# Two transformer blocks with experts on one core: conditioning on VectorE, joined biases, gate in the rows, and a changed start and end of the second experts

## The chip, the cores and the metric

The kernel runs on one core of one Trainium2 chip. The metric is the time of one execution on the device, in microseconds (us). PE is the matrix engine, PEld its weight load, DVE the vector engine, ACT the scalar engine, POOL the general engine, and SP the engine that here only issues transfers.

## What is computed

`reference` runs `first_block` and then `second_block` on 256 tokens of width 1024 (the first block also on 256 context tokens). Cut to what the change touches:

```python
def first_block(x, c, ctx, c_ctx, ...):
    mod_lat = split(silu(c) @ w_mod + b_mod, 6)          # 1024 x 6144
    mod_ctx = split(silu(c_ctx) @ w_mod + b_mod, 6)
    h = rmsnorm(x) * (1 + mod_lat[1]) + mod_lat[0]
    x = x + mod_lat[2] * token_mixer(h, ...)              # attention + gated recurrence
    h = rmsnorm(x) * (1 + mod_lat[4]) + mod_lat[3]
    x = x + mod_lat[5] * moe_ffn(h, ...)                  # 32 experts, top 4 of 32
    return rmsnorm(x, final_norm_g)

def expert(xb, e):                                        # inside moe_ffn
    gu = xb @ w_gate_up[e] + b_gate_up[e]                 # 1024 x 2048
    act = swiglu(gu)
    return act @ w_down[e] + b_down[e]                    # 1024 x 1024

def second_block(x, c, ...):
    mod = silu(c) @ w_ada + b_ada                         # 1024 x 6144
    x = x + gt1 * mixer2(modulate(rmsnorm(x), sh1, sc1))
    x = x + gt2 * hier_moe(modulate(rmsnorm(x), sh2, sc2))  # 32 experts of 256, top 2
    shf, scf = split(silu(c) @ w_ada_f + b_ada_f, 2)      # 1024 x 2048
    return modulate(rmsnorm(x), shf, scf)
```

The last block's context rows are not needed, so the first experts work on the 256 tokens alone.

## The kernel before

All weights are read once from device memory, in tiles of 128 x 2048 fp32 (1 MB) that `wload` (L311) issues from SP into a ring of slots; a tile can be issued when the last reader of its slot is done. Outside the expert stages the ring has five slots. Five stages follow one another.

**Block 1** runs the projections of the token mixer, four pairs of recurrence heads, and attention. `tproj` takes one weight tile: ACT casts it to a high part (`wsh`, L495), DVE takes the rest (`wsl`, L496), and PE multiplies three times (L508 to L510). Work items stand in a queue, `self.q`; `step` runs the first and issues the loads of the first two. Conditioning rows are items of the same queue: `mod` loads two tiles and `modrow` multiplies the condition vector with them on PE (16 matmuls into `modps`, L367), and DVE adds the result to `rowall` (L369). Twenty such rows are listed in `MODS1` and mixed between the projections: twelve go with the head pairs, eight with the last group of gate projections, `g8s`. Four more, for the final norm (`wadaf`), are made at the start of block 2. `mod_cols` turns rows into columns at the end of block 1. `bcast_rows` (L425) copies a row to all partitions by one fp32 matmul.

**The first experts**, `moe1`, go through 32 experts with up to 64 tokens each. An expert takes eight tiles of `wgu` and four of `wdn`. `expert1a` multiplies the gathered tokens (`gu`, L1327), adds the bias by four fp32 matmuls of 32 rows (L1402) and makes the activation; `expert1b` multiplies with `wdn` (`y`, L1358) and adds its bias by two more. `combine` weighs y (`yhi` on ACT, L1236, `ylo` on DVE, L1237), puts the rows back to tokens on PE (`co`, L1248), multiplies by the gate on DVE (L1253) and adds to x (L1254). The next expert's `gu` matmuls are interleaved with the last steps of the present one. The ring has 14 slots here: five of the main ring, one and eight of two other pools. After expert 11 `overflow` asks whether any expert has more tokens than its places; nine tiles of the next expert are issued ahead of this check. The branch isn't taken with this data.

**Block 2** is the second mixer. **The second experts**, `moe2`, run 32 small experts (three 1 MB tiles each: `w1e`, `w3e`, `w2e`), eight with fixed places first, then in an order by their counts: `sorted_places` computes that order as `inv`, and SP reads it into registers (`TENSOR_LOAD`, L1461) before it can issue the loads of a sorted expert. An overflow check lies behind the eight fixed experts. The sums over experts stay in four banks of PSUM (`sum`, L1562).

**The end** (L1607 to L1616) multiplies the sums by the gate, adds x, takes the mean of squares (ACT, L1609), the inverse root through a logarithm and an exponential (L431, L432), scales, adds the shift and writes out.

```python
        for k in range(8):                        # cut: one gu chain of expert1a, then its biases
            nc.tensor.matmul(gu[j][64 * s:64 * s + 64, :], g[:, k, c0:c0 + 64],
                             w[:, ...], start=(k == 0), stop=False)
        for j in range(2):
            for s in range(2):
                bias(gu[j][64 * s:64 * s + 64, :], 0, 1024 * s + 512 * j)
```

Of the kernel before, what the change touches and what calls it, by code (L numbers as in the profile page):

```python
# [23 lines left out]
MODS1 = [(1, j) for j in range(4, 12)] + [(2, j) for j in range(12)]  # L24
NWS, NU, NV = 8, 32, 20
NWR = 5
# [5 lines left out]
def _cols(a):  # L32
# [8 lines left out]
VOFF = {}  # L41
# [14 lines left out]
def _khalf(w):  # L56

    t = w.shape[1] // 512
    return np.ascontiguousarray(w.reshape(2, 4, 128, t, 512).transpose(3, 0, 2, 1, 4)).reshape(2 * t, 128, 2048)
# [62 lines left out]
def layout(i):  # L122
# [117 lines left out]
class Ker:  # L240
    def __init__(self, tc, d, out, dbg=None, stop=None, start=1):
        self.tc, self.nc, self.d, self.out = tc, tc.nc, d, out
        self.dbg = dbg or {}
        self.stop, self.start = stop, start
# [5 lines left out]
    def run(self):  # L250
        with ExitStack() as es:
            tc = self.tc
            self.cp = es.enter_context(tc.tile_pool(name="const", bufs=1))
            self.wp = es.enter_context(tc.tile_pool(name="wts", bufs=NWR))
# [3 lines left out]
            own = self.own = [(self.wp, "w")]  # L258
# [3 lines left out]
            if self.start <= 1:  # L262
                with tc.tile_pool(name="t1late", bufs=1, side="right") as pl, tc.tile_pool(name="t1", bufs=1) as p:
                    self.early = lambda n: p.tile([128, 512], F32, name=n, tag="u", bufs=NU)
                    self.consts()
                    route = self.block1(p, pl, xtile)
            else:
                self.early = lambda n: self.cp.tile([128, 512], F32, name=n)
                self.consts()
                self.x1 = xtile("x").rearrange("p a (b n) -> p (a b n)", b=1).rearrange("p (b n) -> p b n", b=2)  # L270
                self.nc.sync.dma_start(self.x1, self.d['xin'])
                self.add(*(self.mod(2, j) for j in range(12)))
                self.drain()
                self.mod_cols((12, 10, self.mcol2[:, 0:40]))
# [1956 lines left out]
```

## Time and profile before

| | us |
|---|---|
| median of 3 runs | 2112.69 (2109.07 to 2114.51) |
| profiled execution | 2111.07 |
| its span | 2109.3 |
| PE busy in the span | 1945.5 (92%) |
| DVE busy | 896.0 (42%) |
| ACT busy | 511.6 (24%) |

The mean granted clock of PE is 0.963. The span is the time from the first to the last instruction that the profiler recorded. Busy shares are means over stages that have different limits, so the stages have to be read apart. Matmuls are pipelined: a row that says 600 ns for one does not mean that PE issued the next one 600 ns later; where rows stand back to back, the distance of their starts is the price.

### The profile page before, as it was taken

How to read it: one execution, taken by the hardware profiler on the slowest of the kernel's cores; microseconds unless marked ns; L12 is line 12 of the kernel's file. 1: busy time of each engine (PE TensorE's matmuls, PEld its weight loads, DVE VectorE, ACT ScalarE, POOL GpSimd, SP SyncE). 2: the span in 40 equal slices, each digit the busy share in tenths (PEclk: the TensorE clock that was granted, in tenths of full speed). 3: DMA queues.
4: the chain of work that ended last, by engine and by line, in shares of the span. 5: the costliest groups of instructions: out<-in, count | busy, mean ns of one | idle time of the engine just before them, and what ended most of it. 6: DMA issues, size and time to landing. Idle time of an engine off the chain costs nothing. (4 is left out here: it accounts for less than half of the span.)

```text
span 2109.3 us, 30791 instructions
## 1 busy us (share of the span) xinstructions
PE 1945.5 (92%) x12860; PEld 1114.6 (53%) x12861; DVE 896.0 (42%) x1727; ACT 511.6 (24%) x893; POOL 63.3 (3%) x66
## 2 busy tenths in 40 slices
PE   5999999999899999989999999999969998899785
PEld 3888788877733333333333333333338997764331
DVE  5666754445423233332323333242378574421112
ACT  3433454344300001000000100000035543311011
POOL 0000000000000000000000000000032201000000
PEclk9999999999999999989999999999989999989897
DMA  9255636732699999979999999999873133289895
GB/s 362 81 219 201 227 126 258 278 111 80 262 415 427 411 427 416 427 295 407 426 427 427 426 427 427 426 427 427 365 292 124 62 121 103 114 370 420 360 425 226
DMA packets 95272, 646.11 MB, mean 306 GB/s; under 512 B 11668, under 2 KB 12692, under 8 KB 19220
## 3 DMA queue, kind: packets, MB, share of 16 engines
q1 hardware_dynamic: 93296, 642.79, 74.9%
q8 instruction: 104, 1.70, 0.3%
q10 hardware_dynamic: 1828, 1.26, 0.2%
q14 instruction: 44, 0.36, 0.0%
HBM read 642.96 MB, written 1.05 MB: 305 GB/s over the span
## 5 line engine op out<-in xcount | busy, mean ns | idle before, releaser
L1327 PE MATMUL gu<-w,gT 128*64 128x512 f32 x2048 | 481.2, 597 | 0.0
L1327 PEld LDWEIGHTS gu<-w,gT 128*64 128x64 f32 x2048 | 148.1, 137 | 278.1 <-issue 263.1
L1358 PE MATMUL y<-w,aT 128*64 128x512 f32 x1024 | 229.4, 601 | 0.4
L496 DVE TENSOR_TENSOR wsl<-w,wsh 128x1024 fp32r<-128x1024 f32 (+1 forms) x141 | 168.6, 1205 | 97.6 <-ACT wsh L495 97.3
L495 ACT CAST wsh<-w 128x1024 fp32r<-128x1024 f32 (+1 forms) x141 | 143.4, 1030 | 169.0 <-PE tp L509 97.4
L1337 DVE TENSOR_SCALAR act<-gu 128x256 f32<-128x256 f32 x64 | 27.2, 425 | 307.5 <-PE gu L1402 304.2
L1237 DVE SCALAR_TENSOR_TENSOR ylo<-y,sw,yhi 128x512 fp32r<-128x512 f32 x52 | 39.0, 751 | 264.5 <-ACT yhi L1236 264.0
L1358 PEld LDWEIGHTS y<-w,aT 128*64 128x64 f32 x1024 | 71.9, 139 | 148.6 <-issue 143.7
L508 PE MATMUL tp<-hs,wsh 128*128 128x256 f32 (+1 forms) x424 | 139.7, 329 | 0.0
L510 PE MATMUL tp<-hs,wsl 128*128 128x256 f32 (+1 forms) x424 | 134.3, 317 | 4.1 <-DVE wsl L496 4.1
L509 PE MATMUL tp<-hs,wsh 128*128 128x256 f32 (+1 forms) x424 | 133.6, 315 | 0.0
L1529 PE MATMUL ab<-w,gT 128*32 128x256 f32 (+1 forms) x1024 | 99.8, 415 | 17.4 <-DMA w<-in_w1e_dram 10.8
L1236 ACT ACTIVATE yhi<-y,sw 128x512 fp32r<-128x512 f32 x52 | 35.8, 688 | 300.9 <-PE y L1402 239.9
L1253 DVE TENSOR_TENSOR gated<-co,gtb 128x512 f32<-128x512 f32 x128 | 88.3, 690 | 34.6 <-PE co L1248 27.5
L1339 ACT ACTIVATE sge<-act 128x512 f32<-128x512 f32 x32 | 20.1, 630 | 331.3 <-DVE act L1337 331.3
L508 PEld LDWEIGHTS tp<-hs,wsh 128*128 128x128 f32 x424 | 81.7, 193 | 16.3 <-issue 4.9
L1254 DVE TENSOR_TENSOR x<-x,gated 128x512 f32<-128x512 f32 x128 | 88.3, 690 | 3.3
L510 PEld LDWEIGHTS tp<-hs,wsl 128*128 128x128 f32 x424 | 81.6, 193 | 9.9 <-DVE wsl L496 4.9
L508 PE MATMUL tp<-hi,wsh 128*128 128x256 f32 x288 | 85.4, 296 | 0.0
L509 PEld LDWEIGHTS tp<-hs,wsh 128*128 128x128 f32 x424 | 81.8, 193 | 4.5 <-issue 0.7
L1278 PE MATMUL ga<-oh,xhi 128*128 128x256 f32 x208 | 63.5, 333 | 21.9 <-PEq L1292 6.3
L509 PE MATMUL tp<-lo,wsh 128*128 128x256 f32 x288 | 81.7, 284 | 0.0
(576 smaller groups left out, 3099.9 us busy)
## 6 DMA issues: line engine op xcount, KB each, us to landing
w<-in_wgu_dram SPq DMA_DIRECT2D x256, 1024.0 KB, 15.3
w<-in_wdn_dram SPq DMA_DIRECT2D x128, 1024.0 KB, 15.6
w<-in_win_dram SPq DMA_DIRECT2D x50, 1024.0 KB, 5.9
w<-in_w3e_dram SPq DMA_DIRECT2D x32, 1024.0 KB, 14.7
w<-in_w1e_dram SPq DMA_DIRECT2D x32, 1024.0 KB, 11.9
w<-in_w2e_dram SPq DMA_DIRECT2D x32, 1024.0 KB, 15.9
w<-in_wada_dram SPq DMA_DIRECT2D x24, 1024.0 KB, 6.4
w<-in_wmod_dram SPq DMA_DIRECT2D x16, 1024.0 KB, 6.0
```

The source lines that it names most:

```text
L495: nc.scalar.copy(hi, src)
L496: nc.vector.tensor_sub(lo, src, hi.bitcast(F32))
L508: nc.tensor.matmul(out, a[0], b[0], start=first, stop=False)
L509: nc.tensor.matmul(out, a[0], b[1], start=False, stop=False)
L510: nc.tensor.matmul(out, a[1], b[0], start=False, stop=last)
L1237: nc.vector.scalar_tensor_tensor(lo, y, w, hi.bitcast(F32), op0=OP.mult, op1=OP.subtract)
L1253: nc.vector.tensor_mul(part, o[s], gate[:, cs])
L1254: nc.vector.tensor_add(x[:, b, cs], x[:, b, cs], part)
L1278: nc.tensor.matmul(ps[:, 256 * kk:256 * kk + 64 * n], xs[i][:, b, 128 * (k + kk):128 * (k + kk) + 128], ohv[b], start=(b + i == 0), stop=( ...
L1327: nc.tensor.matmul(gu[j][64 * s:64 * s + 64, :], g[:, k, c0:c0 + 64], w[:, 1024 * s + 512 * j:1024 * s + 512 * j + 512], start=(k == 0), s ...
L1358: nc.tensor.matmul(y[64 * s:64 * s + 64, :], aT[:, k % 4, k // 4, :], w[:, o:o + 512], start=(k == 0), stop=False)
L1529: nc.tensor.matmul(ps[m * j:m * j + m, 256 * i:256 * i + 256], g[:, k, c0 + m * j:c0 + m * j + m], w[j][:, k, :], start=(k == 0), stop=(k ...
```

## The change

- **Conditioning on VectorE.** The conditioning weights are laid out transposed, so that a tile holds 256 outputs. `crow` copies the condition vector to all partitions, once per condition, with eight fp32 matmuls and two copies by ACT. `mod` becomes two items of one tile each; an item multiplies the tile by that copy and sums along the row (SCALAR_TENSOR_TENSOR of 128 x 1024 with `accum_out`, L388, twice), and adds the bias (L391). All 48 items, those of the final norm too, are in block 1: 12 with the pairs, 5 with the next projections, 8 with `g8s`, 8 with the four last gate projections, the others between the attention's projections. Items marked light do not count in `step`'s look ahead. `bcast_rows` takes four fp32 matmuls of 128 columns per row.
- **Joined biases.** The two halves of a bias are one fp32r matmul of all 128 rows: three per expert instead of six.
- **Gate in the rows.** y is multiplied by the gate on DVE before it is weighed, in both expert stages; `combine` adds the token sums straight to x.
- **Slots.** The main ring is split into three and two; before each overflow check three more tiles are issued, into the three.
- **Second experts.** `sorted_places` gives `inv` before the gathering matmuls are through; x is added into the sums by four matmuls with the identity behind the overflow check.
- **End.** The squares are taken from the sums, the first table load is placed behind the last activation, and scaling, adding and writing are done in four pieces on two queues.

```diff
-NWR = 5
+NWR, NWB = 3, 2
...
+    def crow(self, p, i):
+
+        nc = self.nc
+        t = p.tile([128, 1024], F32, name="crow", tag="crow")
+        for h in range(2):
+            ps = self.ps("cr")
+            for k in range(4):
+                o = 8 * i + 4 * h + k
+                nc.tensor.matmul(ps[:, 128 * k:128 * k + 128], self.cs[:, o:o + 1].to_broadcast([128, 128]), self.ident, start=True, stop=True)
+            nc.scalar.copy(t[:, 512 * h:512 * h + 512], ps)
+        return t
+
+    def mod(self, p, which, j):
+
+        nc = self.nc
+        src, bias = {1: ('wmod', 'b_mod'), 2: ('wada', 'b_ada_2'), 3: ('wadaf', 'b_ada_f_2')}[which]
+
+        def half(a):
+            def run(w):
+                yield 0
+                key = 0 if which == 1 else 2
+                if self.crows[0] != key:
+                    self.crows = key, self.crow(p, key)
+                c = self.crows[1]
+                o = self.mcol(which, j)
+                for i in range(2):
+                    wi = w[:, 1024 * i:1024 * i + 1024]
+                    n = 2 * a + i
+                    nc.vector.scalar_tensor_tensor(wi, wi, 1.0, c, op0=OP.mult, op1=OP.mult, accum_out=o[:, n:n + 1])
+                o = o[:, 2 * a:2 * a + 2]
+                b = VOFF[bias] + 4 * j + 2 * a
+                nc.vector.tensor_add(o, o, self.vec[:, b:b + 2])
+            return Item(lambda: self.wload(self.d[src][2 * j + a]), run, True)
+        return [half(0), half(1)]
...
-            r = self.msrc(*key)[1]
-            nc.tensor.matmul(ps, self.fold[:, r:r + 1].to_broadcast([128, 128]), self.rowall, start=True, stop=True)
+            for g in range(4):
+                nc.tensor.matmul(ps[:, 128 * g:128 * g + 128], self.mcol(*key)[:, g:g + 1].to_broadcast([128, 128]), self.ident, start=True, stop=True)
...
+            if n == 2:
+                break
...
-        lastg = [self.add(tproj(win[24 + i], LAT, g7)) for i in range(4)][-1]
+        lastg = [self.add(*mixed([tproj(win[24 + i], LAT, g7)], 2)) for i in range(4)][-1]
...
-                self.add(tproj(d['wqb'][4 + i // 2], QS, qrope, nk=6, n=1536))
-            self.add(tproj(d['wqb'][i], QS, keep(qn, "qn"), nk=6, n=1536))
+                self.add(*mixed([tproj(d['wqb'][4 + i // 2], QS, qrope, nk=6, n=1536)], 2))
+            self.add(*mixed([tproj(d['wqb'][i], QS, keep(qn, "qn"), nk=6, n=1536)], 2))
             heads.append(self.add(keysvals(i)))
+            self.add(*(mods.pop(0) for _ in range(1 if i < 3 else len(mods))))
...
-                part = p.tile([128, 512], F32, name="gated", tag="gated", bufs=1)
-                nc.vector.tensor_mul(part, o[s], gate[:, cs])
-                nc.vector.tensor_add(x[:, b, cs], x[:, b, cs], part)
+                nc.vector.tensor_add(x[:, b, cs], x[:, b, cs], o[s])
...
-            for s in range(2):
-                bias(gu[j][64 * s:64 * s + 64, :], 0, 1024 * s + 512 * j)
+            bias(gu[j], 0, 512 * j)
...
-            bias(y[64 * s:64 * s + 64, :], 1, 512 * s)
-        self.combine(p, x, y, oT, wv, gate)
+        bias(y, 1, 0)
+        part = p.tile([128, 512], F32, name="gated", tag="gated", bufs=1)
+        nc.vector.tensor_mul(part, y, gate)
+        self.combine(p, x, part, oT, wv)
...
-        def bias_of(pick):
+        def bias_of(one):
+
+            rows = p.tile([128, 128], F32R, name="brow", tag="brow", bufs=2)
+            nc.vector.tensor_scalar(rows, blk, one, None, op0=OP.mult)
+
             def bias(o, which, c):
-                j, c = (2, c) if which else divmod(c, 1024)
-                r = slice(32 * j, 32 * j + 32)
-                nc.tensor.matmul(o, pick(r, j).to_broadcast([32, 64]), brows[r, c:c + 512], start=False, stop=True)
+                bias_parts()
+                nc.tensor.matmul(o, rows, brow[which][:, c:c + 512], start=False, stop=True)
             return bias
...
-                first = {(e + 1, j): fetch(e + 1, j, spare if j < NW2X else ahead) for j in range(NW2 + NW2X)}
+                free = [spare] * NW2X + [ahead] * NW2 + [self.main] * NWR
+                first = {(e + 1, j): fetch(e + 1, j, free[j]) for j in range(12)}
...
+        order = self.sorted_places(p, sel, pm, count, off)
+        next(order)
...
+            if e0 == 0:
+                inv = next(order)
...
-                request([(n_, q) for n_ in ('w1e', 'w3e') for q in range(e0 + n, e0 + n + 4)])
+                request([(n_, q) for n_ in ('w1e', 'w3e', 'w2e') for q in range(e0 + n, e0 + n + 4)])
                 self.overflow(p, exc, self.caps, pmP, cwP, xs, A, B, late, 2, inv)
+                for b in range(2):
+                    for s in range(2):
+                        nc.tensor.matmul(sums[b][s], self.ident, x[:, b, 512 * s:512 * s + 512], start=False, stop=False)
...
-        nc.scalar.preload_act_table_set("natural_log_exp_and_others")
+        with tc.issue_after(self.last_sig.ins):
+            nc.scalar.preload_act_table_set("natural_log_exp_and_others")
         xo = p.tile([128, 2, 1024], F32, name="xo", tag="xhi")
         for b in range(2):
             for s in range(2):
                 cs = slice(512 * s, 512 * s + 512)
-                nc.vector.tensor_mul(xo[:, b, cs], sums[b][s], gtb[:, cs])
-                nc.vector.tensor_add(x[:, b, cs], x[:, b, cs], xo[:, b, cs])
-                nc.scalar.activation(xo[:, b, cs], x[:, b, cs], AF.Square, accum_out=st[:, b, s:s + 1])
-        self.dump('x4', x)
-        for b in range(2):
+                nc.scalar.activation(xo[:, b, cs], sums[b][s], AF.Square, accum_out=st[:, b, s:s + 1])
             nc.vector.tensor_add(st[:, b, 2:3], st[:, b, 0:1], st[:, b, 1:2])
             self.rstd_from(st[:, b, 3:4], st[:, b, 2:3], 1024, self.eps)
-            nc.vector.scalar_tensor_tensor(xo[:, b, :], x[:, b, :], st[:, b, 3:4], gs, op0=OP.mult, op1=OP.mult)
-            (nc.gpsimd if b == 0 else nc.vector).tensor_add(xo[:, b, :], xo[:, b, :], shb)
-            nc.sync.dma_start(self.out.rearrange("o (b p) n -> p (o b) n", p=128)[:, b, :], xo[:, b, :])
+        for b in range(2):
+            for s in range(2):
+                cs = slice(512 * s, 512 * s + 512)
+                nc.vector.scalar_tensor_tensor(xo[:, b, cs], sums[b][s], st[:, b, 3:4], gs[:, cs], op0=OP.mult, op1=OP.mult)
+                nc.vector.tensor_add(xo[:, b, cs], xo[:, b, cs], shb[:, cs])
+                (nc.sync if s else nc.scalar).dma_start(self.out.rearrange("o (b p) n -> p (o b) n", p=128)[:, b, cs], xo[:, b, cs])
...
-        mods = [self.mod(3, j) for j in range(4)]
-        self.add(*mods)
-        for m in mods[:2]:
-            m.ready, m.w = True, m.prep()
```

The order of instructions moves at four places. First DVE in block 1, ahead of the first recurrence's copy `yh`, before (`wsl` is the cast of a weight tile, `rowall` the conditioning rows):

```order
L742 TENSOR_TENSOR tot<-f 128x256
L742 TENSOR_TENSOR tot<-tot 128x128 x2
L717 TENSOR_TENSOR ksum<-K 128x512
L700 SCALAR_TENSOR_TENSOR qT<-tp,qT 128x512
L718 TENSOR_TENSOR Qb<-qT,f 128x512
L719 TENSOR_TENSOR Qf<-qT,f 128x512
L369 TENSOR_TENSOR rowall<-rowall,modps 128x512
L496 TENSOR_TENSOR wsl<-w,wsh 128x1024 x2
L783 COPY yh<-av 128x512
```

and now (`mcol` holds the conditioning columns, `crow` the copied condition):

```order
L388 SCALAR_TENSOR_TENSOR w,mcol_99<-w,crow 128x1024
L730 TENSOR_TENSOR ksum<-K 128x512
L731 TENSOR_TENSOR Qb<-qT,f 128x512
L732 TENSOR_TENSOR Qf<-qT,f 128x512
L388 SCALAR_TENSOR_TENSOR w,mcol_99<-w,crow 128x1024 x2
L391 TENSOR_TENSOR mcol_99<-mcol_99,vec 128x2
L388 SCALAR_TENSOR_TENSOR w,mcol_99<-w,crow 128x1024
L509 TENSOR_TENSOR wsl<-w,wsh 128x1024
L391 TENSOR_TENSOR mcol_99<-mcol_99,vec 128x2
L388 SCALAR_TENSOR_TENSOR w,mcol_99<-w,crow 128x1024 x2
L796 COPY yh<-av 128x512
L391 TENSOR_TENSOR mcol_99<-mcol_99,vec 128x2
L509 TENSOR_TENSOR wsl<-w,wsh 128x1024
```

The add of one conditioning row has become pairs of multiplications that stand between the casts. PE in the first experts, from one expert's y to the next one's gu, before:

```order
L1358 MATMUL y<-w,aT 64x512 x16
L1402 MATMUL y<-brows,fc 64x512 x2
L1327 MATMUL gu<-w,gT 64x512
L1248 MATMUL co<-yhi,oT 128x512 x2
L1248 MATMUL co<-ylo,oT 128x512 x2
L1248 MATMUL co<-yhi,oT 128x512 x2
L1248 MATMUL co<-ylo,oT 128x512 x2
L1327 MATMUL gu<-w,gT 64x512 x7
```

and now:

```order
L1373 MATMUL y<-w,aT 64x512 x16
L1442 MATMUL y<-brb,brow 128x512
L1343 MATMUL gu<-w,gT 64x512
L1266 MATMUL co<-yhi,oT 128x512 x2
L1266 MATMUL co<-ylo,oT 128x512 x2
L1266 MATMUL co<-yhi,oT 128x512 x2
L1266 MATMUL co<-ylo,oT 128x512 x2
L1343 MATMUL gu<-w,gT 64x512 x7
```

The bias is one matmul of 128 rows instead of two of 64, and the place of the sums `co`, behind one gu matmul pair, is the same. PE at the start of the second experts, the end of the gathering matmuls `ga`, before:

```order
L1278 MATMUL ga<-oh,xhi 128x256
L1278 MATMUL ga<-oh,xlo 128x256
L1278 MATMUL ga<-oh,xhi 128x256
L1278 MATMUL ga<-oh,xlo 128x256
L1529 MATMUL ab<-w,gT 64x256 x9
L1174 MATMUL kc<-ones,sel 32x1 x2
L1529 MATMUL ab<-w,gT 64x256 x15
L1183 MATMUL inv<-gt,off 32x32
```

and now:

```order
L1294 MATMUL ga<-oh,xhi 128x256
L1294 MATMUL ga<-oh,xlo 128x256
L1294 MATMUL ga<-oh,xhi 128x256
L1294 MATMUL ga<-oh,xlo 128x256
L1200 MATMUL inv<-gt,off 32x32
L1294 MATMUL ga<-oh,xhi 128x256
L1294 MATMUL ga<-oh,xlo 128x256
```

The matmul that gives `inv` stood behind 24 projections `ab` and stands now between the gathering matmuls. SP at the end of block 2, up to the first read of `inv`, before:

```order
L311 DMA w<-in_wout_dram 128x2048 x4
L311 DMA w<-in_w3e_dram 128x2048 x2
L311 DMA w<-in_w1e_dram 128x2048 x2
L311 DMA w<-in_w3e_dram 128x2048 x2
L311 DMA w<-in_w2e_dram 128x2048 x2
L311 DMA w<-in_w1e_dram 128x2048 x2
L1461 TENSOR_LOAD inv
L1461 ISA x2
L1461 TENSOR_LOAD inv
```

and now:

```order
L302 DMA w<-in_wout_dram 128x2048 x4
L302 DMA w<-in_w3e_dram 128x2048 x2
L302 DMA w<-in_w2e_dram 128x2048
L302 DMA w<-in_w1e_dram 128x2048 x2
L302 DMA w<-in_w3e_dram 128x2048 x2
L302 DMA w<-in_w2e_dram 128x2048 x2
L302 DMA w<-in_w1e_dram 128x2048 x2
L1500 TENSOR_LOAD inv
```

One `w2e` tile is issued before the first `w1e` tiles, and eleven tiles instead of ten stand ahead of the read.

## Rows read from the trace of the kernel before

**Rows 1.** Stretches: from:to, length, busy us of PE, PEld, DVE, ACT, POOL; PEclk, DMA share, GB/s.

```profile
0.00:339.30 339.30, 312.67 (x2081) 255.39 (x2083) 212.71 (x507) 154.29 (x308) 3.77 (x14) 0.97 0.53 201
339.30:437.30 98.00, 93.84 (x741) 79.76 (x739) 45.90 (x53) 37.60 (x47) 0.00 (x0) 1.00 0.75 275
437.30:580.00 142.70, 135.15 (x826) 102.55 (x826) 66.91 (x170) 57.78 (x119) 0.00 (x0) 0.96 0.40 149
580.00:1535.00 955.00, 922.74 (x4568) 332.04 (x4568) 316.04 (x553) 79.38 (x127) 0.22 (x2) 0.98 0.98 412
1832.00:2090.00 258.00, 216.98 (x1727) 111.95 (x1726) 54.21 (x154) 40.10 (x77) 0.00 (x0) 0.92 0.93 383
```

**Rows 2.** Groups of instructions by line and form, 0 to 590 us.

```profile
L367 PE MATMUL modps<-w,cpad 128*32 128x512 f32 x320 | 39.3, 600 | 0.0
L369 DVE TENSOR_TENSOR rowall<-rowall,modps 128x512 f32<-128x512 f32 x24 | 16.4, 684 | 26.4 <-PE modps L367 26.2
```

**Rows 3.** A group of DVE, whole span; two rows of the timeline, PE and ACT.

```profile
L1138 DVE SCALAR_TENSOR_TENSOR xlo<-x,rs,xhi 128x1024 fp32r<-128x1024 f32 x4 | 4.9, 1278 | 0.0
...
1559.61 2.06 PE L1710 MATMUL xT<-fc,xh 128*128 128x128 f32 x8 [0.38 <-ACT hi L1715]
...
2094.69 0.19 ACT L1609 ACTIVATION_READ_ACCUMULATOR xo<-x 128x1 f32 x1
```

**Rows 4.** One expert's period on PE's timeline, then L1253's group, then a stretch.

```profile
690.10 1.07 PE L1402 MATMUL y<-brows,fc 32*64 32x512 f32 x4
691.10 1.07 PE L1327 MATMUL gu<-w,gT 128*64 128x512 f32 x2
...
810.80 1.07 PE L1327 MATMUL gu<-w,gT 128*64 128x512 f32 x2
...
1537.12 0.50 PE L1248 MATMUL co<-ylo,oT 64*128 64x512 f32 x2
...
L1253 DVE TENSOR_TENSOR gated<-co,gtb 128x512 f32<-128x512 f32 x128 | 88.3, 690 | 34.6 <-PE co L1248 27.5
...
600.00:650.00 50.00, 49.75 (x234) 16.44 (x229) 13.55 (x24) 3.60 (x6) 0.00 (x0) 1.00 1.01 427
```

**Rows 5.** SP's waits from 600 to 900, SP's timeline, and two stretches.

```profile
SPq L311 <- PE gu L1327: 153.0, 78, 6.7
...
914.49 14.08 SPq L311 DMA_DIRECT2D w<-in_wgu_dram  x8
...
941.20 10.05 SPq L311 DMA_DIRECT2D w<-in_wgu_dram  x8
...
1515.88 3.76 SPq L311 DMA_DIRECT2D w<-in_wadaf_dram  x3
...
910.00:915.00 5.00, 5.00 (x26) 1.47 (x22) 0.08 (x1) 0.00 (x0) 0.00 (x0) 1.00 0.01 3
...
1525.00:1530.00 5.00, 4.70 (x20) 2.06 (x22) 3.75 (x6) 0.25 (x1) 0.00 (x0) 0.62 0.04 16
```

**Rows 6.** Timeline behind the last of the first experts: start, us, instruction.

```profile
1534.47 1.07 PE L1402 MATMUL y<-brows,fc 32*64 32x512 f32 x4
1536.33 0.73 PE L1248 MATMUL co<-yhi,oT 64*128 64x512 f32 x3 [0.79 <-ACT yhi L1236]
...
1543.28 0.69 DVE L1254 TENSOR_TENSOR x<-x,gated 128x512 f32<-128x512 f32 x1
```

**Rows 7.** PE's timeline, conditioning rows at block 2's start.

```profile
1561.60 2.56 PE L367 MATMUL modps<-w,cpad 128*32 128x512 f32 x16
```

**Rows 8.** SP's waits from 1780 to 1900 (total, times, longest), and a stretch.

```profile
SPq L1461 <- DVE inv L1185: 21.2, 1, 21.2
...
1855.00:1860.00 5.00, 4.04 (x33) 2.43 (x29) 1.95 (x8) 1.11 (x3) 0.00 (x0) 0.99 0.00 2
```

**Rows 9.** Timeline of the end, behind the last sum.

```profile
2100.73 3.25 DVE L1615 TENSOR_TENSOR xo<-xo,shb 128x1024 f32<-128x1024 f32 x1
2102.92 1.49 SPq L1616 DMA_DIRECT2D out_dram<-xo  x2
```

More of the change, by code (lines that the diff above doesn't have):

```diff
@@ L23 @@
 FIXED, WIDE = 4, 8
-MODS1 = [(1, j) for j in range(4, 12)] + [(2, j) for j in range(12)]
+MODS = [(1, j) for j in range(4, 12)] + [(2, j) for j in range(12)] + [(3, j) for j in range(4)]
 NWS, NU, NV = 8, 32, 20
-NWR = 5
+NWR, NWB = 3, 2
 NS4 = 23
@@ L261, in run @@
             self.last_sig = None
[L262 to L268, printed above, removed]
-                self.consts()
[L270 to L274, printed above, removed]
+            with tc.tile_pool(name="t1late", bufs=1, side="right") as pl, tc.tile_pool(name="t1", bufs=1) as p:
+                self.early = lambda n: p.tile([128, 512], F32, name=n, tag="u", bufs=NU)
+                self.consts()
+                route = self.block1(p, pl, xtile)
             if self.stop == 1:
@@ L351, in v, with mcol @@
         return self.vec[:, o:o + 1]
-    def msrc(self, which, j):
-        src, r = {1: ('wmod', j), 2: ('wada', 12 + j), 3: ('wadaf', 24 + j)}[which]
-        return [self.d[src][2 * j + a] for a in range(2)], r
+    def mcol(self, which, j):
+        return {1: self.mcol1[:, 0, :], 2: self.mcol2, 3: self.mcol3}[which][:, 4 * j:4 * j + 4]
     def modrow(self, cpad, r, pieces):
@@ L452, in step @@
         it = self.q[0]
-        for i in self.q[:2]:
+        n = 0
+        for i in self.q:
             if not i.ready:
                 i.ready, i.w = True, i.prep()
+            n += not i.light
+            if n == 2:
+                break
         if it.gen is None:
@@ L876, in block1 @@
                     self.later(4 * i, lambda i=i: readout(i))
-                self.add(*(tproj(win[28 + a], LAT, keep(qa, "qa", 3, qnorm)) for a in range(3)),
-                         tproj(win[31], HS, keep(ckv, "ckv", 2, cnorm)), tproj(d['wrope'], HS, keep(kr, "kr"), nb=1, n=1024))
+                self.add(*mixed([*(tproj(win[28 + a], LAT, keep(qa, "qa", 3, qnorm)) for a in range(3)),
+                                 tproj(win[31], HS, keep(ckv, "ckv", 2, cnorm)), tproj(d['wrope'], HS, keep(kr, "kr"), nb=1, n=1024)]))
                 est = 10.3 + 30.7
@@ L1193, in sorted_places @@
         nc.vector.tensor_sub(over, po[:, 0:32], self.caps)
-        return perm, inv, pmP, self.excess(p, over)
+        yield perm, pmP, self.excess(p, over)
     def by_place(self, p, t, perm, name):
@@ L1504, in late @@
                                      start=(k == 0), stop=(k == 1))
-            self.combine(p, x, y, self.spread(p, ohv, 2), w, gtb, 2)
+            part = p.tile([128, 512], F32, name="gated", tag="gated", bufs=2)
+            for s in range(2):
+                r = slice(64 * s, 64 * s + 64)
+                nc.vector.tensor_mul(part[r, :], y[r, :], gtb[r, 512 * s:512 * s + 512])
+            self.combine(p, x, part, self.spread(p, ohv, 2), w, 2)
         sums = [[self.pg("sum") for _ in range(2)] for _ in range(2)]
@@ L1581, in moe2 @@
                     cw = cw()
-                    perm, inv, pmP, exc = self.sorted_places(p, sel, pm, count, off)
+                    perm, pmP, exc = next(order)
                     cwP = self.by_place(p, cw, perm, "cwP")
```

127 lines of the change are left out of this document (66 added, 61 removed), and 3 rows, old and new, of the table VECS.

## The prediction

> **What bounds the kernel now.** I read the table of stretches first. The span falls into five stages, and the reader is to see in [rows 1] that no engine bounds all of them. In block 1 (0 to 580 us) PE is busy in 312.67 of the first 339.30 us, in 93.84 of the next 98.00 and in 135.15 of the last 142.70; DVE has 212.71, 45.90 and 66.91. In the first experts (580 to 1535) PE has 922.74 of 955.00 us and the DMA share is 0.98: two resources end together. In the second experts (1832 to 2090) DMA leads, 0.93, and PE has slack. So a microsecond of PE is worth a microsecond in block 1, only as much as DMA allows in the first experts, and nothing in the second.
>
> Then I went from stage to stage: in block 1 to the groups of lines that the change removes; in the first experts to the timeline of PE around one expert, to what SP waited for and when it issued; then to the start of the second experts and to the last 20 us. The sum is made against the profiled execution, 2111.07 us, which is 1.6 us below the median of the runs, 2112.69.
>
> **Block 1, conditioning on VectorE.** Twenty conditioning rows leave PE: 39.3 us of L367 [rows 2]. For that PE makes the condition row twice, 16 fp32 matmuls of 128x128; eight took 2.06 us [rows 3], so 4.1 us. DVE loses 20 adds of 0.684 us, 13.7 us, and gets 96 multiply-and-sum instructions of 128x1024. Their accumulating form is not in the trace. The nearest row is the same operation on the same size without the sum, L1138, 1278 ns [rows 3], some 1.24 us in a back-to-back pair. ACT shows what reading a sum can add: 0.19 us behind each square [rows 3]. So 1.24 to 1.43 us; I take 1.35, between the two, and a DVE bill of 130 us with the small adds.
>
> What that does depends on where the 96 lie in DVE's order: 40 come ahead of the last recurrence's copy (339.3 us in the trace of before), 37 from there to the first attention scores (437.3 us), 19 behind.
> - First stretch: PE loses 12 rows, 12 x 1.97 (39.3/20) = 24 us, and gains 2 for the first condition row; DVE rises from 212.71 to 212.7 + 54 + 3 - 8 = 262 of about 319 us. It is not the bound, but its queue is in order: each instruction that waits for a weight tile holds the wsl casts that PE needs. I take 5 us for that: -17.
> - Second stretch: the stretch would fall by 8 x 1.97 to about 82 us by PE and its idle time, while DVE goes to 45.9 + 37 x 1.35 + 3 - 5.5 = 93 us. DVE becomes the bound; with little idle time that is 95 to 98 us. DMA moved 27 MB here (0.75 share) [rows 1]; up to eight tiles more is 35 MB, 83 us at 427 GB/s [rows 4], under DVE. Gain about 2.
> - Third stretch: 19 x 1.35 = 26 us on a DVE with 76 us free, but ahead of softmax steps that PE waits for; I take +5.
>
> Together -14, with -35 (all of PE's saving) and +10 (DVE's queue costs 5 us more in the outer stretches and 14 in the second) as ends.
>
> **First experts.** Per expert PE spends 1.0 us on the y bias (691.10 - 690.10) [rows 4] and twice that, by count of matmuls, on the gate-up bias. Three fp32r matmuls of 128x512 take their place; two took 0.50 us [rows 4], so 0.75. That frees 2.25. Against it stands one more step in the chain from y to the sums: the gate is now multiplied into y on DVE (0.69 us by L1253 [rows 4]) before yhi. One gu pair, 1.0 us, covers the present chain; the extra 0.7 is a stall of PE. Net 29.9 (119.7/4 between the two gu rows of [rows 4]) - 2.25 + 0.7 = 28.4 us. DMA needs 12 tiles of 1.049 MB at 427 GB/s, 29.5 us. So PE, now 0.4 us above DMA per expert, falls 1.1 below it, and SP's waits for gu tiles, 153.0 us in 78 waits [rows 5], lose their reason. After this the stage is DMA's.
>
> Its worth is the DMA time lost now: 412 GB/s over the 955 us of the stage [rows 1] are 393 MB, which take 921 us at 427 GB/s, so 34 us are lost. About 10 of them lie behind the last tiles (0.04 share from 1525 to 1530 [rows 5]), where DMA has nothing to do. Ten more lie at the overflow check, where SP had to wait until 914.49 for slots (0.01 share from 910 to 915) [rows 5]; a PE that is not behind has freed them. The restart at 941.20, after the check, stays: the three extra prefetched tiles go out before it, and all must have landed then, so about 4 us remain. I take DMA's end 20 us earlier. The tail then shortens too: three wadaf tiles (issued from 1515.88 on [rows 5], 7.4 us) end where DMA falls idle, near 1525, so the last expert tile landed near 1517.5, and PE finished y at 1535.5 [rows 6]. This backlog of 18 us falls by 7, because PE is no longer behind. Behind it the four gate multiplications (L1253) go, which alternate with the adds up to 1543.97 [rows 6]: -3 with the new step subtracted. In all -30; ends -8 (the overflow gap alone) and -36.
>
> **Block 2.** Two rows of 16 conditioning matmuls on its path, 2.56 us [rows 7] and a like one, go, with 8 MB of loads before the projection tiles: -4, ends 0 and -6. The broadcast rows become four fp32 matmuls each instead of one: 1 us for 0.6, twice or so on the path; nothing.
>
> **Second experts.** SP stood 21.2 us at inv; DMA moved 2 GB/s from 1855 to 1860 [rows 8]. In the new order inv comes behind eight gather matmuls instead of 24 projections, some 15 us earlier, so this hole of some 6 us closes; the third early w2e tile is worth one tile, 2.4 us. SP's wait before the first of these loads is for a pool's release and stays, as does the restart behind the second overflow check, with eight more register reads hidden by the queued tiles. -9, ends 0 and -12. The four matmuls that add x are on PE beside loads: nothing; if that cover were gone, 2.5 us.
>
> **The end.** The last y gets the gate step, +1. Then four multiply-add pairs on DVE go; the squares read PSUM at once; one of two table loads moves off the path; the two adds on POOL and DVE at once, 3.25 us, become four of 0.69 us on DVE, with four output transfers on two queues [rows 9]. Last issue some 4 us earlier: -4, ends -1 and -6.
>
> Sum: -14 - 30 - 4 - 9 - 4 = -61: 2050 on the profiled execution, **2052** on the median.
>
> **Rivals.**
> 1. *The accumulating multiply runs at half rate*, because it reads two fp32 tiles and an accumulator: 2.48 us each. Against it: no DVE row on two SBUF tiles is slow without a cause beside it. For it: no row accumulates. DVE would have 45.9 + 92 + 3 - 5.5 = 135 us in the second stretch, 142 with gaps (+44), be at 307 of 339 in the first (+10) and delay attention by 10: block 1 +64, the kernel 2111 + 64 - 47 = 2128, **slower**. It decides from about 2.2 us on, where block 1 loses the 47 that the rest gains. [...] The trace's rows without a sum, 1.28 us for 1024 columns, do not show a halved rate. Chance 0.07.
> 2. *The first experts stay with PE.* The longer chain from y stalls PE by 2 us, not 0.7; then only the overflow gap and the last adds go: 2052 + 20 = 2072, and 2081 if the second experts keep their hole too. For it: the stall of 0.79 us before co [rows 6] shows what happens without cover. Chance 0.18.
> 3. *Block 1 gives all that PE is spared*, since DVE and its loads run ahead in every stretch: 2052 - 21 = 2031. Against it: 93 us of DVE against 82 of PE in the second stretch. Chance 0.12.
> 4. *The conditioning holds DVE's queue*: block 1 +10 instead of -14: 2076. Chance 0.13.
>
> **Numbers.** The forecast has 0.50, within 2040 to 2064. The range is 2028 to 2085: it holds rivals 2 to 4 and leaves out the first and the far ends. A difference of 0.3% (6.3 us) is what a measurement can tell from none. Slower by that: 0.05, rival 1 at its full price; the same: 0.03, rival 1 at a lower one; faster: 0.92.
>
> **What would show it.** Right: the new instruction at 1.25 to 1.45 us; DVE busier than PE only from the last recurrence to the first scores; L1402's place at 0.75 us per expert; four gu starts 118 us apart, with PE idle for DMA and no long waits of SP for gu; no 2 GB/s hole after 1830; the last issue within 11 us of the last sum. Wrong: a conditioning multiply above 2 us, block 1 longer than 580 us, or an expert's period still above 29.8 us.

## The result and the profile after

The changed kernel takes 2054.82 us in the median (2051.94 to 2057.06), the kernel before 2112.83 beside it: a ratio of 0.9727, 95% interval 0.9707 to 0.9748. The forecast was 2052, and the time lies 3 us above it. But the sum came out by luck: some 15 us too little gain in block 1 and 16 too much in the first experts cancel, and 9 too much in the second experts is only partly made up elsewhere. The table of stretches of the changed kernel (an execution of 2057.06 us) shows it, cut at the same events in block 1 as [rows 1], the first experts from their first gu to their last y, then the block behind them, the second experts from the first w1e request, and the end (the columns are those of [rows 1]):

```profile
0.00:323.40 323.40, 296.72 (x1961) 261.08 (x1963) 253.31 (x599) 157.85 (x314) 3.08 (x12) 0.97 0.53 193
323.40:411.30 87.90, 78.34 (x573) 73.75 (x572) 77.57 (x133) 33.70 (x43) 0.00 (x0) 0.94 0.91 341
411.30:546.60 135.30, 129.78 (x828) 101.45 (x827) 88.11 (x213) 57.81 (x118) 0.00 (x0) 0.98 0.62 227
546.60:1495.40 948.80, 878.64 (x4295) 333.89 (x4294) 257.25 (x505) 82.26 (x131) 0.00 (x0) 0.98 1.00 415
1500.80:1785.70 284.90, 254.62 (x2868) 233.46 (x2869) 182.82 (x268) 133.26 (x197) 54.99 (x51) 0.93 0.28 103
1785.70:2044.70 259.00, 216.75 (x1766) 114.94 (x1765) 66.11 (x172) 43.20 (x85) 0.00 (x0) 0.92 0.92 378
2044.70:2055.30 10.60, 0.00 (x0) 0.00 (x0) 5.45 (x10) 1.97 (x10) 0.00 (x0) 0.72 0.27 100
```

The same cuts of the kernel before are at 339.3, 437.3, 576.0, 1535.5, 1544.0, 1832.4, 2090.0 and 2109.3. The difference by stage, beside the forecast:

| stage | before | after | change | forecast |
|---|---|---|---|---|
| block 1, to the last recurrence | 339.3 | 323.4 | -15.9 | -17 |
| to the first scores | 98.0 | 87.9 | -10.1 | -2 |
| to the first gu | 138.7 | 135.3 | -3.4 | +5 |
| first experts, to the last y | 959.5 | 948.8 | -10.7 | -27 |
| last sums of these | 8.5 | 5.4 | -3.1 | -3 |
| block 2 | 288.4 | 284.9 | -3.5 | -4 |
| second experts | 257.6 | 259.0 | +1.4 | -8 (with the gate's +1) |
| end | 19.3 | 10.6 | -8.7 | -5 |

The changes sum to -54.0, the distance of the two spans (2109.3 and 2055.3), for a forecast of -61.

The new instruction, groups of DVE by form (columns as in [rows 3]), then two of its kind back to back on DVE's timeline:

```profile
L388 DVE SCALAR_TENSOR_TENSOR w<-w,crow 128x1024 f32<-128x1024 f32 x96 | 115.2, 1219 | 3.8 <-DMA w<-in_wmod_dram 3.7
L388 DVE DVE_READ_ACCUMULATOR w<-w,crow 128x1 f32 x96 | 8.0, 83 | 0.0
...
L1154 DVE SCALAR_TENSOR_TENSOR xlo<-x,rs,xhi 128x1024 fp32r<-128x1024 f32 x4 | 4.9, 1274 | 0.0
...
L1944 DVE TENSOR_SCALAR th<-th 128x1024 f32<-128x1024 f32 x1 | 0.7, 695 | 0.0
```

```profile
376.75 1.22 DVE L388 SCALAR_TENSOR_TENSOR w<-w,crow 128x1024 f32<-128x1024 f32 x1
377.90 0.08 DVE L388 DVE_READ_ACCUMULATOR w<-w,crow 128x1 f32 x1
377.90 1.22 DVE L388 SCALAR_TENSOR_TENSOR w<-w,crow 128x1024 f32<-128x1024 f32 x1
```

The sum costs nothing: the accumulating form takes 1219 ns, not more than L1154 without it (1274), and its read of 0.08 us starts together with the next one, 1.15 us after the last (377.90 - 376.75). What a second source costs is less clear: L1944, with one source of the same size, takes 695 ns (L1729, also with one, 1558), so the second source may cost some 0.5 us (1219 - 695), with or without a sum. The kernel before has such a row too (L1898, 694 ns), which I had not set beside the 1278 when I wrote that its rows show no halved rate. No run here settles that.

In the first experts, behind the overflow check, the loads now end last, but four experts take as long as before: two gu rows of PE's timeline, four experts apart, stand 119.5 us apart (119.7 in [rows 4]). SP waits for loads that are under way, no longer for PE (total, times, longest, from 900 to 1500, against [rows 5]):

```profile
1012.99 1.07 PE L1343 MATMUL gu<-w,gT 128*64 128x512 f32 x2
...
1132.49 1.07 PE L1343 MATMUL gu<-w,gT 128*64 128x512 f32 x2
```

```profile
SPq L302 <- DMA w<-in_wgu_dram: 302.3, 143, 4.6
SPq L302 <- DMA w<-in_wdn_dram: 147.2, 69, 4.6
SPq L302 <- PE y L1373: 25.1, 10, 15.2
```

So PE did fall below the loads; the loads became slower by as much. In the changed kernel they move 419 to 420 GB/s in this stage, against 427 in [rows 4].

Ahead of the overflow check SP still waits for PE (waits from 500 to 900), and PE sets the pace. There the two gu rows of [rows 4], four experts apart, stand 115.5 us apart instead of 119.7, 28.9 per expert (115.6 in the run e6 below, whose loads move 427 GB/s there). SP's waits, rows of that stretch up to the pair that ends it, and two rows of the kernel before:

```profile
SPq L302 <- PE gu L1343: 86.7, 55, 7.2
```

```profile
654.61 1.07 PE L1343 MATMUL gu<-w,gT 128*64 128x512 f32 x2
...
720.74 0.73 PE L1442 MATMUL gu<-bra,brow 128*128 128x512 f32 x2
721.40 7.09 PE L1373 MATMUL y<-w,aT 128*64 128x512 f32 x32
...
728.85 1.07 PE L1343 MATMUL gu<-w,gT 128*64 128x512 f32 x2
...
732.21 3.22 PE L1343 MATMUL gu<-w,gT 128*64 128x512 f32 x13
...
769.71 0.50 PE L1442 MATMUL y<-brb,brow 128*128 128x512 f32 x1
770.14 1.07 PE L1343 MATMUL gu<-w,gT 128*64 128x512 f32 x2
```

```profile
768.19 1.07 PE L1327 MATMUL gu<-w,gT 128*64 128x512 f32 x2
...
770.77 1.51 PE L1327 MATMUL gu<-w,gT 128*64 128x512 f32 x6
```

The joined biases take 0.66 us (720.74 to 721.40) and 0.43 us (769.71 to 770.14). From the first gu pair to the next, with the sums between them, it takes 3.36 us (728.85 to 732.21) instead of 2.58 (768.19 to 770.77): the gate's step stalls PE by 0.78 us.

In the second experts the hole of [rows 8] is gone and another stands 55 us behind the first request: no load from 1840 to 1845 with PE busy throughout, while SP waits for a y matmul to let go of a slot (waits of SP from 1786 to 1850):

```profile
1840.00:1845.00 5.00, 5.00 (x46) 2.85 (x44) 2.01 (x5) 1.10 (x2) 0.00 (x0) 1.00 0.00 0
```

```profile
SPq L302 <- PE y L1600: 18.4, 2, 14.3
```

### The profile page after: what moved, and what is told of

The parts are those of the page before. It is cut to its first block, busy times and chain, and to the rows that moved or that the text cites. A ratio compares the mean times of both kernels' runs of the same rounds, so it can differ in the third digit from the quotient of the medians.

```text
span 2055.3 us, 29728 instructions
## 1 busy us (share of the span) xinstructions
PE 1856.3 (90%) x12292; PEld 1119.2 (54%) x12293; DVE 934.5 (45%) x1903; ACT 512.9 (25%) x897; POOL 58.1 (3%) x63
## 5 line engine op out<-in xcount | busy, mean ns | idle before, releaser
L1343 PEld LDWEIGHTS gu<-w,gT 128*64 128x64 f32 x2048 | 156.3, 137 | 266.5 <-issue 232.9
L1373 PE MATMUL y<-w,aT 128*64 128x512 f32 x1024 | 234.8, 601 | 13.3 <-DMA w<-in_wdn_dram 12.5
L1254 ACT ACTIVATE yhi<-gated,sw 128x512 fp32r<-128x512 f32 x52 | 37.5, 721 | 328.0 <-DVE gated L1376 249.9
L388 DVE SCALAR_TENSOR_TENSOR w<-w,crow 128x1024 f32<-128x1024 f32 x96 | 115.2, 1219 | 3.8 <-DMA w<-in_wmod_dram 3.7
L1376 DVE TENSOR_TENSOR gated<-y,gtb 128x512 f32<-128x512 f32 x32 | 22.1, 692 | 183.1 <-PE y L1442 183.1
L1270 DVE TENSOR_TENSOR x<-x,co 128x512 f32<-128x512 f32 x128 | 79.4, 683 | 19.3 <-PE co L1266 19.3
L523 PE MATMUL tp<-hi,wsl 128*128 128x256 f32 x288 | 82.7, 287 | 0.0
## 6 DMA issues: line engine op xcount, KB each, us to landing
w<-in_wgu_dram SPq DMA_DIRECT2D x256, 1024.0 KB, 19.9
w<-in_wdn_dram SPq DMA_DIRECT2D x128, 1024.0 KB, 19.9
w<-in_w3e_dram SPq DMA_DIRECT2D x32, 1024.0 KB, 15.9
w<-in_w2e_dram SPq DMA_DIRECT2D x32, 1024.0 KB, 19.6
```

Source lines behind the costliest of these rows:

```text
L388: nc.vector.scalar_tensor_tensor(wi, wi, 1.0, c, op0=OP.mult, op1=OP.mult, accum_out=o[:, n:n + 1])
L523: nc.tensor.matmul(out, a[1], b[0], start=False, stop=last)
L1254: nc.scalar.activation(hi, y, AF.Identity, scale=w)
L1270: nc.vector.tensor_add(x[:, b, cs], x[:, b, cs], o[s])
L1373: nc.tensor.matmul(y[64 * s:64 * s + 64, :], aT[:, k % 4, k // 4, :], w[:, o:o + 512], start=(k == 0), stop=False)
```

## The experiments

The open questions were why the loads slowed, whether DVE has the room that block 1's gain suggests, and what the parts are worth one by one.

**Is the slower rate the chip's, or the loads in flight?** Three kernels: the two unchanged ones on the same chip, and one with fewer slots.

> The kernel before, unchanged, on the same chip as the next three runs. In the first experts the trace shown first moved 427 GB/s with some 15 us from issue to landing; the changed kernel moved 419 to 420 with 20 us. Theory (the rate falls because more loads are in flight): 427 GB/s here again and 420 in the next run. Rival (another chip, another rate): this run and the next one move the same, whichever it is.

> The changed kernel, unchanged. Theory of more loads in flight: 420 GB/s in the first experts, 2.50 us a tile, span near 2055. Rival of the chip: the rate of the run before this one; if that is 427, the first experts end 15 us earlier and the span is near 2038.

> The changed kernel with 11 slots instead of 14 in the first experts (five instead of eight in the second pool, nine instead of twelve tiles ahead of the overflow check). Fewer loads can be in flight. Theory of more loads in flight: from issue to landing 12 to 16 us, 424 to 427 GB/s in the steady stretch, four experts in 118 us instead of 119.5. Rival: still 419 to 420 GB/s, 119.5 us, and a few us lost at the start and at the overflow check, where fewer tiles are prefetched (+3 to +10 us in the whole).

```diff
-NW2, NW2X, NW2B = 8, 1, 8
+NW2, NW2X, NW2B = 5, 1, 8
...
-                first = {(e + 1, j): fetch(e + 1, j, free[j]) for j in range(12)}
+                first = {(e + 1, j): fetch(e + 1, j, free[j]) for j in range(len(free))}
```

Measured: 2109.99, 2057.34 and 2068.78 us. The chip falls as a cause: the stretch from 1100 to 1200 us of the first run, then of the second:

```profile
1100.00:1200.00 100.00, 97.71 (x488) 36.12 (x486) 37.13 (x64) 8.57 (x14) 0.00 (x0) 0.98 1.01 427
```

```profile
1100.00:1200.00 100.00, 92.52 (x457) 36.07 (x453) 24.95 (x49) 8.08 (x13) 0.00 (x0) 0.98 1.01 420
```

The third run did not test what it should: with 11 slots a load still took 19.9 us from issue to landing and the rate stayed at 419 to 420; only the prefetch was shorter (+11 us). That left another difference: where the slots lie. The change adds columns to the table of vectors and drops other tiles ahead of the slots. Before, the first slot of the main ring starts at byte 33024 of a partition, 129 x 256, and the other slots of the first experts at multiples of 256 too; in the changed kernel it starts at 31520, which is 32 above a multiple of 256, and so do the others. The traces hold no addresses. But the tiles ahead of the slots in the two kernels differ by 1504 bytes, as these two addresses do, which is 32 short of six times 256.

**Do the slots' addresses set the rate?**

> The changed kernel with 32 bytes of padding in each of two pools, so that every weight slot starts at a multiple of 64 bytes per partition (they start at 32 above one in the changed kernel, in the first experts; in the kernel before at multiples of 256). Nothing else moves. Theory A64 (a tile that starts off a 64-byte line is written slower): 426 to 427 GB/s in the first experts, 2.454 us a tile, four experts in 118 us, the whole 14 to 18 us shorter, near 2040. Theory A256 (the line is 256 bytes; the slots now start 64 above one): as the changed kernel, 419 to 420 GB/s. Rival (the rate is set by something else in the change, the loads in flight or what DVE and ACT do): 419 to 420 GB/s, no change in time.

> As the run before with padding of 224 and 96 bytes: every weight slot starts at a multiple of 256 bytes, as in the first experts of the kernel before. A64 and A256: 426 to 427 GB/s, near 2040. Rival: 419 to 420 GB/s, near 2057.

> The kernel before with 32 bytes of padding ahead of the slots, which then start 32 above a multiple of 256. A64 and A256: 419 to 420 GB/s in the first experts; a tile takes 2.495 us, an expert 29.9, as long as PE needs there, so the time grows by less than the loads do: 3 to 12 us, near 2117. Rival: 427 GB/s and 2110.

```diff
+        pad = cp.tile([128, 56], F32, name="pad")
+        nc.gpsimd.memset(pad, 0.0)
...
+        pad = p.tile([128, 24], F32, name="pad2")
+        nc.gpsimd.memset(pad, 0.0)
         off = p.tile([128, 97], F32, name="off")
```

That is e6; e5 has 8 columns in both places, e7 has 8 in the first alone. Measured: 2047.75 us for e5, 2036.64 for e6 (ratio 0.9640 to the kernel before, 0.9624 to 0.9656), 2111.29 for e7 (1.0001, 0.9991 to 1.0011). The same stretch of e5, e6 and e7:

```profile
1100.00:1200.00 100.00, 92.56 (x455) 36.05 (x451) 27.75 (x55) 8.69 (x14) 0.00 (x0) 0.98 1.01 421
```

```profile
1100.00:1200.00 100.00, 91.74 (x458) 35.25 (x456) 27.87 (x54) 9.07 (x15) 0.00 (x0) 1.00 1.01 427
```

```profile
1100.00:1200.00 100.00, 97.52 (x486) 35.76 (x482) 36.30 (x63) 8.67 (x14) 0.00 (x0) 0.98 1.01 419
```

The rate follows the address in all five kernels, whatever else is in them: 427 at a multiple of 256, 421 at 64 above one, 419 to 420 at 32 above one. Adding 32 bytes to the kernel before brings the slow rate, and padding the changed kernel to 256 takes it away. How many loads are in flight does not set it: in e6 a load takes 19.6 us from issue to landing (issues from 1100 to 1300, median), about as long as in e3, and the rate is 427.

```profile
w<-in_wgu_dram SPq DMA_DIRECT2D x57, 1024.0 KB, 19.6
```

A64 falls. A256 stands in the main, though it forecast no gain for e5: that is 7 to 10 us faster than the changed kernel's runs (2054.82 and 2057.34), so 64 above is a little better than 32 above, and no run is at 128. The padding also moves some tiles behind it that are no slots; no run moves those alone. Beside 427 GB/s the loads are slower by 1.4% at 64 above (421) and by 1.6 to 1.9% at 32 above (420 and 419); no run shows why. In e6 the first experts take 930.2 us to the last y (545.9 to 1476.1), 29.3 less than before. In e7 I had expected 3 to 12 us more; the slower loads cost nothing, because PE needs 29.9 us per expert there, as much as they do.

**Has DVE room in block 1?**

> The changed kernel with one more multiplication of 128x1024 ahead of each conditioning one, which leaves the tile as it is: 96 more instructions of 1.15 us on DVE, 110 us, the price that a half rate would have had. Theory (block 1 has room on DVE except from the last recurrence to the first scores): that stretch goes from 88 to 120-125 us, the stretch before it gains 5 to 15, the one after it 3 to 10; the whole +40 to +55. Rival (DVE has room everywhere, the stretch is held by loads and PE): +10 to +20. Rival (DVE's in-order queue holds PE everywhere): +90 or more.

```diff
                 for i in range(2):
...
+                    nc.vector.scalar_tensor_tensor(wi, wi, 1.0, wi, op0=OP.mult, op1=OP.max)
                     nc.vector.scalar_tensor_tensor(wi, wi, 1.0, c, op0=OP.mult, op1=OP.mult, accum_out=o[:, n:n + 1])
```

Measured: 2108.15 us, +51 against e2. The three stretches of block 1:

```profile
0.00:338.60 338.60, 300.58 (x1975) 263.81 (x1977) 288.52 (x631) 157.97 (x314) 3.09 (x12) 0.95 0.50 181
338.60:447.30 108.70, 82.78 (x559) 76.92 (x557) 108.42 (x155) 32.71 (x42) 0.00 (x0) 0.86 0.73 261
447.30:599.70 152.40, 136.94 (x827) 105.79 (x826) 122.64 (x257) 58.35 (x121) 0.00 (x0) 0.94 0.62 226
```

The whole agrees, the places less: +14, +21 and +17 us (324.4, 86.9 and 136.2 in e2, by the first matmul into the scores, which starts 1 us ahead of the cut here). In the middle stretch DVE is busy in 108.42 of 108.70 us and is the bound, as the theory says, but it grew by less than the 32 to 37 us that I had expected, and the last stretch by more than 3 to 10. In the last one DVE has 30 us free and the stretch still grows by 17: PE's waits sum to 15.4 us there instead of 5.3 in e2, 2.8 of them for a softmax step on DVE (`pr`) and 5.4 for a cast on ACT, and PE is busy for 6 us more, at a mean granted clock of 0.94 instead of 0.98. At this price of the conditioning the whole gain of the change is gone (0.9993, 0.9981 to 1.0004), where my first rival put a loss of 17 us.

**What are the joined biases worth?**

> The changed kernel with the expert biases of the first experts as they were: six fp32 matmuls of 32 rows instead of three fp32r matmuls of 128. Theory (joining them is what brought PE below the loads): an expert needs 28.5 + 2.2 = 30.7 us of PE against 29.9 of loads, SP waits for PE again, and the first experts grow by 15 to 25 us. Rival (loads at 420 GB/s hide the biases either way): within 5 us.

```diff
-            bias(gu[j], 0, 512 * j)
+            for s in range(2):
+                bias(gu[j][64 * s:64 * s + 64, :], 0, 1024 * s + 512 * j)
...
-        bias(y, 1, 0)
+        for s in range(2):
+            bias(y[64 * s:64 * s + 64, :], 1, 512 * s)
```

The rows and `bias_of` are those of the kernel before. Measured: 2069.26 us, some 13 more than the changed kernel; in the profiled executions (spans 2062.3 and 2055.3 us) the first experts are 9 longer (958.1 against 948.8 to the last y). The first twelve experts are 14 longer (353.4 us against 339.4), and the wait at the overflow check is back (a DMA share of 0.03 from 875 to 880). Behind them four experts take as long as with joined biases, by PE's timeline of this run:

```profile
1024.61 1.93 PE L1343 MATMUL gu<-w,gT 128*64 128x512 f32 x6
...
1144.09 1.93 PE L1343 MATMUL gu<-w,gT 128*64 128x512 f32 x6
```

119.5 us again. The stretch from 1100 to 1200 us, and SP's waits from 1020 to 1400:

```profile
1100.00:1200.00 100.00, 96.61 (x483) 35.45 (x480) 28.57 (x52) 8.78 (x14) 0.00 (x0) 0.98 1.01 419
```

```profile
SPq L302 <- PE gu L1343: 61.8, 45, 3.6
```

PE is busier than in e2 (96.61 against 92.52), and SP waits for it at times (1.6 us in the changed kernel): with the biases apart PE needs 29.9 us per expert, level with the loads at 420 GB/s (12 tiles in 30.0), so that behind the check they cost nothing. Neither expectation holds in size: my 30.7 us of PE was 0.8 too high. Joining the biases is worth 1.0 us of PE per expert (29.9 against 28.9), not 2.25 less the stall. e8 shows the two together: with the biases apart three gu pairs, not one, stand ahead of the sums (x6 above, x2 in the changed kernel), which covers the gate's step.

**What are the other parts worth?** Four kernels on top of e6.

> The kernel of e6_align256 with nine instead of eight slots of the second pool in the second experts. Theory (the hole in the loads some 55 us after the first request, 5 to 7 us, is there because PE still holds every slot): one more slot of 2.45 us shortens the hole by that, the whole by 2 to 3 us against e6, near 2034. Rival (PE sets the pace there, and the slot only moves the hole): no change, 2036.6.

> The kernel of e6_align256 with the matmul and copy that give the sorted places back behind the first projections of the second experts. Theory (the early places closed one hole in the loads and PE's slots opened another of the same size, so they brought nothing): the first hole, 5 to 6 us, comes back about 20 us after the first request, the later one shrinks to under 2 us, and the whole stays within 2 us of 2036.6. Rival (the early places are worth the hole they closed): +5 to +7 us.

> The kernel of e6_align256 with the gate of the first experts behind the sums again, four multiplications on DVE per expert as before. Theory (at 29.45 us of loads per expert PE has 1 us to spare, so the step is hidden, and only the tail behind the last expert counts): the first experts' period stays 117.8 us per four, the last sums take 8 instead of 5 us, the whole +2 to +4. Rival (the gate ahead of yhi stalls PE by 0.7 us in every expert and that counts): -5 to -15.

> The kernel of e6_align256 with the preload of the activation table not tied to the last gate activation, as it was before. Theory (both table loads of the end were taken off the path by placing one preload): two loads of 1.28 us stand behind the squares again, and from the last sum to the end are 13 instead of 10.6 us. Rival (one load was on the path): 12 us.

```diff
-NW2, NW2X, NW2B = 8, 1, 8
+NW2, NW2X, NW2B = 8, 1, 9
```

```diff
-        next(order)
...
-            if e0 == 0:
-                inv = next(order)
...
-                    perm, pmP, exc = next(order)
+                    next(order)
+                    inv = next(order)
+                    perm, pmP, exc = next(order)
```

```diff
-        part = p.tile([128, 512], F32, name="gated", tag="gated", bufs=1)
-        nc.vector.tensor_mul(part, y, gate)
-        self.combine(p, x, part, oT, wv)
+        self.combine(p, x, y, oT, wv, gate=gate)
```

```diff
-        with tc.issue_after(self.last_sig.ins):
-            nc.scalar.preload_act_table_set("natural_log_exp_and_others")
+        nc.scalar.preload_act_table_set("natural_log_exp_and_others")
```

(The second is e10; the third e11, cut: the four multiplications are back in `combine`, and the gate is copied as in the kernel before; the last e12.)

- e9: 2034.24 us (2036.64 in e6), the second experts 253.5 us against 257.1. The later hole is shorter, the stretch of e6 and then the one of e9 that hold it:

```profile
1817.00:1822.00 5.00, 5.00 (x41) 3.51 (x41) 1.09 (x3) 0.37 (x1) 0.00 (x0) 1.00 0.56 231
1822.00:1827.00 5.00, 5.00 (x46) 2.90 (x44) 2.30 (x6) 1.11 (x2) 0.00 (x0) 1.00 0.00 0
```

```profile
1815.00:1820.00 5.00, 5.00 (x46) 3.46 (x46) 1.09 (x3) 0.37 (x1) 0.00 (x0) 1.00 0.82 341
1820.00:1825.00 5.00, 5.00 (x46) 3.00 (x44) 2.76 (x6) 1.10 (x2) 0.00 (x0) 1.00 0.06 16
```

  The two rows and the one behind them hold some 7.4 us without loads in e6 and 6.0 in e9 (five us times one minus the share), so the hole is 1.4 us shorter, not 2.45. This fits the theory in place, and in the sign. The time alone would not show it, nor the stage: it differs by up to 3 us between runs of one kernel.
- e10: 2037.84 us; the second experts take 256.3 us, not more than e6's 257.1. The waits of SP from 1765 to 1830 show the first hole back beside the second, and so do three stretches:

```profile
SPq L302 <- PE y L1603: 18.4, 2, 14.3
SPq L1502 <- DVE inv L1204: 18.0, 1, 18.0
```

```profile
1785.00:1790.00 5.00, 4.55 (x41) 2.86 (x36) 1.74 (x8) 0.75 (x2) 0.00 (x0) 1.00 0.37 157
1790.00:1795.00 5.00, 3.98 (x33) 2.13 (x34) 1.99 (x10) 0.73 (x2) 0.00 (x0) 0.91 0.71 285
...
1820.00:1825.00 5.00, 5.00 (x45) 2.95 (x43) 2.43 (x6) 1.11 (x2) 0.00 (x0) 1.00 0.28 116
```

  The first hole is worth 4.6 us, and the second shrinks from 7.4 us in e6 to 3.9 (I had expected under 2). Their sum, 8.5, is 1 us more than in e6. The early places are worth nothing here: what they let SP issue sooner only fills the slots sooner that PE holds until the same y.
- e11: 2043.16 us, +6.5. The first experts are no longer than in e6 (929.9 to the last y, 930.2), the last sums take 8.1 us instead of 5.4: as expected. The whole was to be 2 to 4 us longer; most of the remaining 4 us lies behind them, in block 2 and the second experts together (545.7 against 543.0), where a wait of SP for a small load of constants is 9.0 us instead of 1.6; why is open, and it says nothing on the gate.
- e12: 2042.33 us, a single run. Behind the squares two loads of tables stand again, and the end takes 13.3 us instead of 10.6, by the timeline of its end:

```profile
2028.61 1.28 ACT L442 ACT_TABLE_LOAD   x1
...
2030.40 1.28 ACT L443 ACT_TABLE_LOAD   x1
```

The version with aligned slots, e6, and the one with a slot more on top of it, e9, beat both kernels: 0.9640 and 0.9648 of the kernel before (0.9624 to 0.9656 and 0.9634 to 0.9662), which doesn't tell the two apart.

## Why the prediction was right, and where it was not

- *Block 1, -14: measured -29.4.* The failing steps are the second and the third stretch; the first was right (-15.9 for -17; DVE waited 3.7 us for conditioning tiles there, by L388's row, where I had taken 5 for the casts behind them). The term that was too large is the price of the new instruction: 1.35 us, measured 1.15 from start to start, so 96 x 0.20 = 19 us of DVE that are not there. The 2.48 us of my first rival, half of the rate, no run shows: the 1.15 us stand in their place. DVE has 77.57 us in the second stretch, not 93; half of the difference is the new instruction (42.1 us for a forecast of 50), the rest is other work, three weight casts among it, that lies elsewhere. PE has 78.34 and the loads a share of 0.91: three resources nearly level, none of them a bound by itself, so "DVE becomes the bound" is the sentence that failed. My +5 for the attention was a -3.4: PE's waits there sum to 5.4 us, less than the 7.5 of the kernel before. What happened is my third rival (a chance of 0.12), to within 6 us.
- *First experts, -27 to the last y: measured -10.7.* PE's part was right in its mechanism and half a microsecond off: 28.9 us per expert for a forecast of 28.4. The stall was sized right (0.78 for 0.7); the three joined biases cost 1.1 us, not 0.75, and what they replace 2.9, not 3.0. The failing step is "DMA needs 12 tiles at 427 GB/s": that rate belonged to the slots' addresses of the kernel before, and a change of the tables ahead of them moved these to 32 bytes above a multiple of 256, where the runs show 419 to 420. With the address put right (e6) the step gives -29.3. My sign of being wrong, an expert's period still above 29.8 us, came true: 119.5/4 is 29.9.
- *The tail, -3: -3.1. Block 2, -4: -3.5.* Right.
- *Second experts, -9: +1.4 with the gate's step.* The hole at inv closed, as forecast. The failing step is that I booked the closed hole as gain without asking what is late next: PE, which holds the slots of the first four experts until y (e10, e9). The changed address may add some to it (e6 takes 257.1); the stage differs by up to 3 us between runs of one kernel (257.6 and 254.7 of the kernel before), so the -9 is missed, but the +1.4 is not told from nothing.
- *The end, -5: -8.7.* I took one table load off the path; both left it, 2.7 us by e12. The squares were undersized too: they end 4.9 us behind the last sum in [rows 3] (2094.69 and 0.19 more, against 2090.0), and 1.3 us behind it now.

```profile
2045.83 0.65 ACT L440 ACTIVATE tn<-tn,eps 128x1 f32<-128x1 f32 x2
2046.38 0.33 ACT L441 ACTIVATE tn<-tn 128x1 f32<-128x1 f32 x2
...
2048.64 2.87 ACTq L1668 DMA_DIRECT2D out_dram<-xo  x2
```

  In the changed kernel's end, above, no table load stands between the squares and the logarithm or between it and the exponential, and the first output leaves 4 us after the last sum.

So the number is right by luck as much as by its reasons. PE's saving in block 1 and in the first experts, the tail, block 2 and the end came as forecast in kind; but 15 us too little in block 1 stand against 16 too much in the first experts, whose cause, an address, was in no term and no rival, and against 9 too much in the second experts.

## What to carry to other kernels

Ask of every load-bound stage at what address its tiles land: tiles that grew or went ahead of them cost 19 us in the first experts here (948.8 against 930.2), and no line of the diff names it. Read the price of an instruction on PE where PE sets the pace, and in the same stretch of both kernels. When a hole in a transfer closes, follow the slots to the next thing that holds them before booking the gain. A stage in which two resources end together gives only the smaller of the two gains.

## What was not expected of the hardware

In the stretch from 1100 to 1200 us, loads of 128 rows of 8192 bytes ran at 427 GB/s into slots that start at a multiple of 256 bytes of a partition (e1, e6), at 421 from 64 above one (e5) and at 419 to 420 from 32 above one (e7, e2). In the changed kernel a multiplication of two fp32 tiles of 128x1024 with a running sum took DVE 1.15 us from start to start and 1219 ns by its row, no more than one without (L1154, 1274 ns), and the read of the sum, 0.08 us, is hidden in it: it starts together with the next multiplication.
